# A fused two-block transformer on one core: TensorE's order at the stage ends, and the start addresses of its operands

## The chip, the cores and the metric

The kernel runs on one core of one Trainium2 chip. The metric is the device time of one launch in microseconds (us). A core has five engines that work beside each other and meet at semaphores: TensorE (in the rows PE, its weight loads PEld), VectorE (DVE), ScalarE (ACT), GpSimd (POOL) and SyncE (SP), which here issues the DMAs. A matmul holds one operand still in the array (the stationary one, at most 128x128) and streams the other one through it (the moving one, up to 512 columns); its result goes to PSUM, of which a core has eight banks of 512 float32 columns.

## The reference, cut to what matters

Two blocks of two layers each on x of 256x1024, batch 1. All matrices are float32 and are read from memory once.

```
for l in range(2):                                   # first block
    x = layer_norm(a*x + 0.5*swiglu(x, ffn1_in[l], ffn1_out[l]))          # f1
    x = layer_norm(a*x + hybrid_mixer(x, ...))                            # m1
    x = layer_norm(a*x + 0.5*swiglu(x, ffn2_in[l], ffn2_out[l]))          # f2
for l in range(2):                                   # second block
    h = rmsnorm(x); x = x + (g0*attn(h) + g1*conv(h) + g2*pool(h)) @ w_o  # m2
    h = rmsnorm(x); x = x + (silu(h@w_gate) * (h@w_up)) @ w_out           # g2

def swiglu(x, w_in, w_out):                          # d_ff = 2816
    gate, up = split(x @ w_in); return (silu(gate) * up) @ w_out
def hybrid_mixer(x, ...):                            # three attentions of 8 heads, 64 wide
    q, k, v, gates = split(x @ w_in)                 # dilated, banded, top-k
    merged = sum(sigmoid(g_i) * (o_i @ w_br_i)); return merged @ w_out
```

## The kernel before, in words

**Number format.** Every float32 operand is split in two: a high part in the matmul's own rounded format (float32r, written by ScalarE, L189) and the rest (VectorE, L190). A product is three matmuls, high by high, high by low, low by high (`mm3`, L229 to L231). In the FFN's input product (`swish_t`, L460 and L462) the activations are the moving operand, 512 columns (high and low side by side) against the weights' high part and 256 against their low part.

**Slabs.** A weight matrix is cut into slabs of 128x1024. `slab` loads one by DMA into one of 4 buffers `raw` and splits it into one of 9 slots `wh` and `wl`. A slab feeds 12 matmuls in every product. The slot comes free when the last of them has run.

**Tiles.** The activations' transpose, split, is one tile `XP` (in the rows xp): 8 blocks of 128 rows, each 256 high columns and 256 low columns. It is the stationary operand of all projections and of the output projection. The FFN's hidden tiles (ht), the attention's outputs (oh, ol) and the convolution's (cvp) are *pages*, rotating buffers of 4 KB per partition; they are the stationary operands of the FFN's output product and of the branches. VectorE, ScalarE and the DMAs are put in order by a scheduler in the build; TensorE's order is the kernel's own.

**TensorE's order.** A planner runs while the program is written. `spend` adds each matmul's expected time to a clock; `later(ns, f)` puts a piece of work (the transposes of a finished tile, an attention head's scores) into a list, due so many ns after now; when the clock passes the due time, the piece is written into TensorE's stream between two matmuls of the running product. `until` and `have` force a piece that is needed. The delays are chosen by hand: they stand for the time that the other engines need until the piece's input is there. Nothing is measured at run time: if the input is late, TensorE stands.

**Stage ends.** A stage ends with a sum over two row tiles t of 128 rows. `finish(t, O)` adds it to x, normalises (VectorE, with one power on GpSimd), and hands the transposes back to XP to `to_xt`, with a delay of 6200, 6500 or 7500 ns. In the FFN the output product of the last `TAIL` = 3 of 11 hidden units is kept for the end, as this sum: for each t, each half n of the columns, each unit u. In the mixers `branch` adds three gated products into M, and `out_project` transposes M and multiplies it by w_out.

**PSUM.** The banks are acc 3, s 2, pt 2 and tp 1. tp takes nearly all transposes and, in `attend`, also the product of weights and values.

**Addresses.** Every partition's memory is given out in the order of declaration. XP starts at byte 16,512, which is 128 past a multiple of 512. The raw, wh and wl buffers (71,456 is the first wh) and all pages (145,184 is the first) start 288 past a multiple of 512.

Of the kernel before, what the change touches and what calls it, by code (L numbers as in the profile page):

```python
# [157 lines left out]
def block_kernel(ctx: ExitStack, tc: tile.TileContext, I, out, stages=ALL):  # L158
# [79 lines left out]
        spend(360)  # L238


    XP = cpool.tile([128, 8, 2, S], F32R, name="xp")
    XH, XL = XP[:, :, 0], XP[:, :, 1]
    X = [cpool.tile([128, D], F32, name=f"x{t}") for t in range(2)]
# [10 lines left out]
    CR = cpool.tile([128, S], F32R, name="cr")  # L254
    SEL = cpool.tile([128, 8], F32R, name="sel")
    mhalf = cpool.tile([128, 8], F32, name="mhalf")
    G.memset(mhalf, -0.5)
    G.memset(CR.bitcast(F32), 0.0)

# [25 lines left out]


    def rope_tables():
        pi = cpool.tile([128, 2], I32, name="posi")
        nc.sync.dma_start(pi, I["pos"])
        pf = cpool.tile([128, 2], F32, name="posf")  # L290
        V.tensor_copy(pf, pi)
        two_pi = 2 * math.pi
        parts, rest = [], two_pi
        for _ in range(3):
            e = math.floor(math.log2(rest)) - 7
            p = math.floor(rest / 2.0 ** e) * 2.0 ** e
            parts.append(p)
            rest -= p
        parts.append(float(np.float32(rest)))
        for t in range(2):  # L300
            rt = tmp.tile([128, 4, 64], F32, tag="sm", bufs=4, name="rt")
            a, kq, b, sc = rt[:, 0, :32], rt[:, 0, 32:], rt[:, 1], rt[:, 2]
            ki = rt[:, 3, :32].bitcast(I32)
            V.tensor_scalar(a, K[:, C_INV:C_INV + 32], pf[:, t:t + 1], None, op0=OP.mult)
            V.tensor_scalar(kq, a, 1.0 / two_pi, None, op0=OP.mult)
            V.tensor_copy(ki, kq)
            V.tensor_copy(kq, ki)
            for p in parts:
                V.scalar_tensor_tensor(a, kq, -p, a, op0=OP.mult, op1=OP.add)
            V.tensor_scalar(b[:, 32:], a, math.pi, -math.pi, op0=OP.min, op1=OP.max)  # L310
            V.tensor_scalar(a, b[:, 32:], -1.0, None, op0=OP.mult)
            V.tensor_tensor(a, a, b[:, 32:], op=OP.max)
            V.tensor_scalar(b[:, :32], a, -1.0, math.pi / 2, op0=OP.mult, op1=OP.add)
            A.activation(sc, b, AF.Sin)
            for v, f in ((0, 1.0), (1, -0.125)):
                V.tensor_scalar(RT[:, v, t, 0, :32], sc[:, :32], f, None, op0=OP.mult)
                V.tensor_scalar(RT[:, v, t, 0, 32:], sc[:, :32], f, None, op0=OP.mult)
                V.tensor_scalar(RT[:, v, t, 1, :32], sc[:, 32:], -f, None, op0=OP.mult)
                V.tensor_scalar(RT[:, v, t, 1, 32:], sc[:, 32:], f, None, op0=OP.mult)
# [113 lines left out]

    def ffn(w_in, w_out, finish, prepare, started=None):
        O, H = {}, {}
        TAIL = 3

        def swish():
            h = tmp.tile([128, 2, 256], F32, tag="ropb", bufs=2, name="h")
# [68 lines left out]
            H[u] = page("op", [128, 2, 2, S], F32R, name="ht")  # L508
            split(H[u][:, 0], H[u][:, 1], p.rearrange("p b t n -> p b (t n)"))

        later(1000, lambda: h_transposes(0))
        later(5000, lambda: h_transposes(1))
        for u in range(2, NU):
            if u == 6:
                if started is not None:
# [11 lines left out]
                            out_mm(v, t, w, n)  # L527
        W = {u: out_slabs(u) for u in range(NU - TAIL, NU)}
        for t in range(2):
            for n in range(2):  # L530
                for u in range(NU - TAIL, NU):
                    out_mm(u, t, W[u], n)
            finish(t, [O[t, 0], O[t, 1]])

# [4 lines left out]
    def attend(heads, vt, vi, pen, period, sinks=None, finished=None):  # L539

        parts = [page("op", [128, 4, S], F32R, name=n) for n in ("oh", "ol")]

        def scores(pr):
            if pr < 3:
                later(period, lambda: scores(pr + 1))
            s, sm = [], []
            for hb in range(2):
                s.append(bank("s"))
                sm.append(tmp.tile([128, 386], F32, tag="sm", bufs=4, name="smx"))
            for t in range(2):  # L550
                for hb in range(2):
                    heads(2 * pr + hb, t, s[hb][:, cols(t)])
            spend(700)
            mn, den = small(4, name="mn"), small(4, name="den")
            for hb in range(2):
                h = 2 * pr + hb
                if sinks is not None:
                    V.tensor_copy(sm[hb][:, 128:386:257], sinks[:, h:h + 1].to_broadcast([128, 2]))
                for t in range(2):
                    i, c = 2 * hb + t, 129 * t  # L560
                    n = 128 * (t + 1)
                    V.tensor_tensor_reduce(
                        out=sm[hb][:, c:c + n], in0=s[hb][:, cols(t)], in1=pen(t), scale=1.0,
                        scalar=3e38 if sinks is None else sinks[:, h:h + 1],
                        op0=OP.add, op1=OP.min, accum_out=mn[:, i:i + 1])
                    if sinks is not None:
                        n += 1
                    A.activation(sm[hb][:, c:c + n], sm[hb][:, c:c + n], AF.Exp,  # L568
                                 bias=mn[:, i:i + 1], scale=-1.0, accum_out=den[:, i:i + 1])
            r = small(4, name="den")  # L570
            V.reciprocal(r, den)
            for hb in range(2):
                for t in range(2):
                    i, c = 2 * hb + t, slice(129 * t, 129 * t + 128 * (t + 1))
                    A.activation(sm[hb][:, c], sm[hb][:, c], AF.Copy, scale=r[:, i:i + 1])
            later(7500, lambda: weights(pr, sm))

        def weights(pr, sm):
            ps = []
            for hb in range(2):  # L580
                p = bank("pt")
                for b, c in enumerate((0, 129, 257)):
                    T.transpose(p[:, b * 128:b * 128 + 128], sm[hb][:, c:c + 128], ident)
                    spend(109)
                pts = tmp.tile([128, 384], F32, tag="pt", bufs=2, name="pts")
                A.activation(pts, p[:, :384], AF.Copy)
                ps.append(pts)
            later(2000, lambda: values(pr, ps))

        def values(pr, ps):  # L590
            p = bank("tp")
            for b in range(2):
                for hb in range(2):
                    v = vt[:, b, vi(2 * pr + hb), :]
                    rows = slice(hb * 64, hb * 64 + 64)
                    if b == 0:
                        T.matmul(p[rows, 0:256], v, ps[hb][:, 0:256], start=True, stop=False,
                                 skip_group_check=True)
                    else:
                        T.matmul(p[rows, 128:256], v, ps[hb][:, 256:384], start=False, stop=True,  # L600
                                 skip_group_check=True)
            spend(700)
            split(parts[0][:, pr], parts[1][:, pr], p[:, :256])
            if pr == 3:
                finished()

        scores(0)
        return parts
# [39 lines left out]
            V.scalar_tensor_tensor(y, g, 1.0, p, op0=OP.add, op1=OP.mult)  # L648
            V.tensor_tensor(m, m, y, op=OP.add)

    def branch(g, slabs, parts, M):

        w = [[slab(slabs[n, s]) for s in range(slabs.shape[1])] for n in range(2)]
        last = 2 * len(w[0]) - 1
        for t in range(2):
            ts = slice(t * 128, t * 128 + 128)
            for n in range(2):
                p = bank("acc")
                for k in range(last + 1):
                    c = slice((k % 2) * 512, (k % 2) * 512 + 512)  # L660
                    mm3(p, (parts[0][:, k, ts], parts[1][:, k, ts]),
                        (w[n][k // 2][0][:, c], w[n][k // 2][1][:, c]), k == 0, k == last)
                merge(g[n][:, t], p, None if M is None else M[n][:, t])

    def out_project(src, M, finish):

        for t in range(2):
            to_xt(t, lambda k, t=t: M[k // 4][:, t, (k % 4) * 128:(k % 4) * 128 + 128], 2500 * t)
        w = [slab(src[s]) for s in range(8)]
        for t in range(2):  # L670
            have(t)
# [7 lines left out]
    def mixer1(l, finish, prepare):  # L679
# [140 lines left out]
        branch(gb, br[1], P["b"], ga)  # L820
        prepare()
        need("c")
        branch(gc, br[2], P["c"], ga)
        out_project(I[f"w_out_{l}"], ga, finish)


    def mixer2(l, finish, prepare):
        w = I[f"w2_in_{l}"]

        def qk(src, which, name):  # L830
            tr = page("qk", [128, 4, S], name=name)

            def evac(t, p):
# [6 lines left out]
                V.tensor_scalar(ss, ss, 1.0 / HD, None, op0=OP.mult)  # L840
                r = rsqrt(ss, 8, 1e-6)
                V.tensor_tensor(qs, qs, r[:, :, None].to_broadcast([128, 8, 64]), op=OP.mult)
                later(5000, lambda: head_transposes(
                    tr, t, qs, scale=qkg[:, 2 * l + which:2 * l + which + 1]))

            return tr, (src, evac, 512)
# [143 lines left out]
        gv = [gates(w[5 + n], "o") for n in range(2)]  # L990
        prepare()
        until(lambda: "o" in ready)
        branch(gv, I[f"w2_attn_{l}"], P["o"], gt)
        out_project(I[f"w2_o_{l}"], gt, finish)


    def rms_row(kind, l):
# [19 lines left out]
    for i, (kind, l) in enumerate(stages):  # L1017
# [14 lines left out]
        def finish(t, O):  # L1032
# [14 lines left out]
                for hs in HALVES:  # L1047
                    nc.sync.dma_start(out[t, :, hs], X[t][:, hs])
            elif row is not None:
                to_xt(t, blocks(rms_norm(t, mv, rows[-1])), 7500 if first else 6500)  # L1050
            else:
                to_xt(t, blocks(X[t]), 6200)

        if kind in ("f1", "f2"):
            ffn(I[f"ffn{kind[1]}_in_{l}"], I[f"ffn{kind[1]}_out_{l}"], finish, prepare,
# [25 lines left out]
```

## Time and profile before

| | |
|---|---|
| median of 3 runs | 2052.9 us (2050.36 to 2054.67) |
| the profiled execution's own time | 2050.83 us |
| its span, first to last instruction | 2049.0 us |
| mean granted clock of TensorE | 0.998 |
| PE busy | 1998.9 us, 98% of the span |
| DVE busy | 1367.4 us, 67% |
| ACT busy | 1072.2 us, 52% |
| DMA queues' packets, share of 16 engines | 53.7% |

A matmul's recorded time (about 0.39 us for 512 columns) is from its issue to its modelled end, and the next one is issued before that. What a matmul costs in a full stream is the step from its start to the start of the next, and that is read from the timeline. A stop shows as idle time in brackets behind the instruction that waited, with the one that ended the wait.

### The profile page before, as it was taken

Reading aid. Unit: us, or ns where it says so; the run is one execution under the profiler, and the core shown is the slowest. Engines: PE = TensorE matmul, PEld = TensorE weight load, DVE = VectorE, ACT = ScalarE, POOL = GpSimd, SP = SyncE. Lnnn points to the kernel's source line nnn. Section 1 sums busy time; section 2 is a strip of 40 time slices with the busy share of each in tenths; the row PEclk is TensorE's granted clock in tenths of the full one; section 3 lists DMA queues with packets and bytes.
Section 4 is the critical chain, followed back from the end, with each engine's and each line's share of the span. In section 5 each row is a group of like instructions: output and inputs, shape, how many; then the busy total and the mean of one; then the engine's idle time right before and its main releaser. Section 6 shows DMA issues by size and latency. Waiting matters only on the chain.

```text
span 2049.0 us, 27340 instructions
## 1 busy us (share of the span) xinstructions
PE 1998.9 (98%) x10216; PEld 1636.2 (80%) x10216; DVE 1367.4 (67%) x2264; ACT 1072.2 (52%) x1767; POOL 33.8 (2%) x34
## 2 busy tenths in 40 slices
PE   8999999999999999999999999899999999999999
PEld 7888867778887888777778887778788878777887
DVE  7767775576667666885567668565666675567664
ACT  6554567635554554457735554574355545534553
POOL 0000000000000000000000000100000010000000
PEclk9999999999999999999999999999999999999999
DMA  8665544456555655543446554445465644555662
GB/s 303 222 186 169 166 134 141 137 176 225 189 191 181 199 189 167 184 139 129 145 155 236 196 185 137 161 154 196 144 206 185 195 147 141 165 175 185 186 192 85
DMA packets 99973, 358.55 MB, mean 175 GB/s; under 512 B 11904, under 2 KB 11904, under 8 KB 99840
## 3 DMA queue, kind: packets, MB, share of 16 engines
q1 hardware_dynamic: 99840, 356.81, 53.7%
q8 instruction: 80, 1.31, 0.3%
q14 instruction: 53, 0.43, 0.1%
HBM read 355.72 MB, written 1.05 MB: 174 GB/s over the span
## 4 chain that ended last, share of the span: by engine, by line
PE 83%; DVE 9%; ACT 4%; issue 2%; DMA 2%; POOL 1%; POOLq 0%; SPq 0%; DVEq 0%; ACTq 0%
PE acc L460 19%; PE acc L229 10%; PE acc L462 10%; PE acc L230 9%; PE acc L231 9%; DVE wl L190 4%; PE s L231 4%; PE s L229 3%; PE s L230 3%; PE pt L231 3%; PE pt L230 3%; PE pt L229 3%; ACT wh L189 2%; PE s L716 1%; ACT smx L568 1%
## 5 line engine op out<-in xcount | busy, mean ns | idle before, releaser
L190 DVE TENSOR_TENSOR wl<-raw,wh 128x1024 fp32r<-128x1024 f32 (+1 forms) x656 | 794.0, 1221 | 408.2 <-ACT wh L189 406.5
L189 ACT ACTIVATE wh<-raw 128x1024 fp32r<-128x1024 f32 (+1 forms) x656 | 683.7, 1055 | 592.2 <-PE pt L231 245.3
L460 PE MATMUL acc<-xp,wh 128*128 128x512 f32 x1728 | 608.9, 394 | 0.0
L462 PE MATMUL acc<-xp,wl 128*128 128x256 f32 x1728 | 482.9, 279 | 0.0
L460 PEld LDWEIGHTS acc<-xp,wh 128*128 128x128 f32 x1728 | 324.1, 188 | 76.6
L229 PE MATMUL acc<-wh,xp 128*128 128x512 f32 (+1 forms) x896 | 367.5, 410 | 6.4 <-ACT wh L189 6.4
L231 PE MATMUL acc<-wh,xp 128*128 128x512 f32 (+1 forms) x896 | 356.6, 398 | 2.5 <-DVE xp L190 2.5
L230 PE MATMUL acc<-wl,xp 128*128 128x512 f32 (+1 forms) x896 | 356.9, 398 | 0.5 <-DVE wl L190 0.5
L462 PEld LDWEIGHTS acc<-xp,wl 128*128 128x128 f32 x1728 | 324.7, 188 | 1.9
L229 PEld LDWEIGHTS acc<-wh,xp 128*128 128x128 f32 x896 | 170.5, 190 | 53.5 <-issue 11.7
L231 PEld LDWEIGHTS acc<-wh,xp 128*128 128x128 f32 x896 | 170.3, 190 | 44.5 <-DVE xp L190 4.7
L230 PEld LDWEIGHTS acc<-wl,xp 128*128 128x128 f32 x896 | 170.6, 190 | 35.9 <-DVE wl L190 1.0
L469 ACT ACTIVATE th<-gu 128x256 f32<-128x256 f32 x108 | 45.1, 417 | 136.5 <-DVE gu L466 136.4
L231 PE MATMUL s<-wh,ht 128*128 128x512 f32 x264 | 103.4, 392 | 0.7
L230 PE MATMUL s<-wl,ht 128*128 128x512 f32 x264 | 103.8, 393 | 0.0
L229 PE MATMUL s<-wh,ht 128*128 128x512 f32 x264 | 103.8, 393 | 0.0
L229 PE MATMUL pt<-wh,ht 128*128 128x512 f32 x264 | 103.2, 391 | 0.0
L231 PE MATMUL pt<-wh,ht 128*128 128x512 f32 x264 | 102.9, 390 | 0.0
L230 PE MATMUL pt<-wl,ht 128*128 128x512 f32 x264 | 102.9, 390 | 0.0
L466 DVE TENSOR_TENSOR gu<-acc,gu 128x256 f32<-128x256 f32 x216 | 90.1, 417 | 3.8 <-ACT gu L465 3.8
L465 ACT ACTIVATE gu<-acc 128x256 f32<-128x256 f32 x216 | 79.2, 367 | 5.4 <-PE acc L462 5.4
L470 DVE SCALAR_TENSOR_TENSOR h<-th,gu 128x256 f32<-128x256 f32 x108 | 45.9, 425 | 48.5 <-ACT th L469 48.5
(243 smaller groups left out, 2171.7 us busy)
## 6 DMA issues: line engine op xcount, KB each, us to landing
raw<-in_w_in_dram SPq DMA_DIRECT2D x184, 512.0 KB, 3.6
raw<-in_ffn_in_dram SPq DMA_DIRECT2D x176, 512.0 KB, 4.2
raw<-in_ffn_out_dram SPq DMA_DIRECT2D x88, 512.0 KB, 3.7
raw<-in_w_ffn_in_dram SPq DMA_DIRECT2D x88, 512.0 KB, 4.3
raw<-in_w_ffn_out_dram SPq DMA_DIRECT2D x44, 512.0 KB, 3.7
raw<-in_w_br_dram SPq DMA_DIRECT2D x24, 512.0 KB, 4.0
raw<-in_w_out_dram SPq DMA_DIRECT2D x16, 512.0 KB, 4.2
raw<-in_w_o_dram SPq DMA_DIRECT2D x16, 512.0 KB, 4.2
```

The source lines that it names most:

```text
L189: A.activation(dst_h, src, AF.Copy)
L190: V.tensor_sub(dst_l, src, dst_h.bitcast(F32))
L229: T.matmul(p, x[0], w[0], start=start, stop=False)
L230: T.matmul(p, x[0], w[1], start=False, stop=False)
L231: T.matmul(p, x[1], w[0], start=False, stop=stop)
L460: T.matmul(p, w[0][:, c], XP[:, k].rearrange("p a n -> p (a n)"), start=k == 0, stop=False, skip_group_check=True)
L462: T.matmul(p[:, 256:], w[1][:, c], XH[:, k], start=False, stop=k == 7, skip_group_check=True)
L465: A.activation(gu[:, i], p[:, 256:], AF.Copy)
L466: V.tensor_tensor(gu[:, i], p[:, :256], gu[:, i], op=OP.add)
L469: A.activation(th, gu[:, 0], AF.Tanh, scale=0.5)
L470: V.scalar_tensor_tensor(h[:, j], th, 1.0, gu[:, 0], op0=OP.add, op1=OP.mult)
L568: A.activation(sm[hb][:, c:c + n], sm[hb][:, c:c + n], AF.Exp, bias=mn[:, i:i + 1], scale=-1.0, accum_out=den[:, i:i + 1])
```

## The change

Seven edits, of which six move work in TensorE's stream and one moves tiles in memory.

- Addresses: two tiles without use (384 and 352 bytes per partition) and two small tiles declared earlier. XP then starts at byte 16,896, the slabs' first wh at 72,192 and the pages at 145,920, all multiples of 512, and so do all raw, wh, wl and page buffers.
- The FFN's kept sum: TAIL is 4, so that 8 slabs stand in the 9 slots for it, and for each t the units run outside and the halves inside.
- The weights-by-values product goes to a pt bank and is due 1000 ns later.
- `branch` itself hands out M's transposes for t when it has finished t (due 3000 ns later); `out_project` no longer does.
- The transposes of q and k in the second block's mixer are due after 9000 ns and not 5000.
- The FFN's first hidden transposes are due 1500 and 2000 ns later.
- After an FFN or a first mixer the transposes to XP are due after 7000 and not 6200 ns (no norm to come), or 10000 and not 7500 (the last FFN of the first block).

```diff
+    cpool.tile([128, 96], F32, name="pad")
     XP = cpool.tile([128, 8, 2, S], F32R, name="xp")
...
+    pi = cpool.tile([128, 2], I32, name="posi")
+    pf = cpool.tile([128, 2], F32, name="posf")
+    cpool.tile([128, 88], F32, name="pad2")
...
-        TAIL = 3
+        TAIL = 4
...
-        later(1000, lambda: h_transposes(0))
-        later(5000, lambda: h_transposes(1))
+        later(2500, lambda: h_transposes(0))
+        later(7000, lambda: h_transposes(1))
...
         for t in range(2):
-            for n in range(2):
-                for u in range(NU - TAIL, NU):
+            for u in range(NU - TAIL, NU):
+                for n in range(2):
                     out_mm(u, t, W[u], n)
...
-            later(2000, lambda: values(pr, ps))
+            later(3000, lambda: values(pr, ps))
         def values(pr, ps):
-            p = bank("tp")
+            p = bank("pt")
...
+            if last:
+                to_xt(t, lambda k, t=t: M[k // 4][:, t, (k % 4) * 128:(k % 4) * 128 + 128], 3000)
-        for t in range(2):
-            to_xt(t, lambda k, t=t: M[k // 4][:, t, (k % 4) * 128:(k % 4) * 128 + 128], 2500 * t)
...
-                later(5000, lambda: head_transposes(
+                later(9000, lambda: head_transposes(
...
-                to_xt(t, blocks(rms_norm(t, mv, rows[-1])), 7500 if first else 6500)
+                to_xt(t, blocks(rms_norm(t, mv, rows[-1])), 10000 if first else 6500)
-                to_xt(t, blocks(X[t]), 6200)
+                to_xt(t, blocks(X[t]), 7000)
```

Three places in TensorE's stream. First, the first layer's dilated attention, behind the first pair of heads (tp and pt are PSUM banks, pts the transposed weights, vx the values, ropa a rotated query that is being transposed, acc a gate's product). Before:

```order
L614 MATMUL tp_2584<-k_75,ropa_2494 128x128 x4
L229 MATMUL acc_2526<-wh_2502,xp_72 128x512
L230 MATMUL acc_2526<-wl_2503,xp_72 128x512
L231 MATMUL acc_2526<-wh_2502,xp_72 128x512
L597 MATMUL tp_2593<-pts_2549,vx_82 64x256
L597 MATMUL tp_2593<-pts_2555,vx_82 64x256
L600 MATMUL tp_2593<-pts_2549,vx_82 64x128
```

And in the changed program:

```order
L616 MATMUL tp_2586<-k_76,ropa_2496 128x128 x4
L229 MATMUL acc_2528<-wh_2504,xp_73 128x512
L230 MATMUL acc_2528<-wl_2505,xp_73 128x512
L231 MATMUL acc_2528<-wh_2504,xp_73 128x512
L229 MATMUL acc_2527<-wh_2516,xp_73 128x512
L230 MATMUL acc_2527<-wl_2517,xp_73 128x512
L231 MATMUL acc_2527<-wh_2516,xp_73 128x512
L599 MATMUL pt_2598<-pts_2551,vx_83 64x256
L599 MATMUL pt_2598<-pts_2557,vx_83 64x256
L602 MATMUL pt_2598<-pts_2551,vx_83 64x128
```

The values stand three matmuls later, and no longer in the bank that the rotated query's transposes have just filled.

Second, the end of the last branch and the start of the output projection in the first mixer (gate is M, s_3938 and s_3940 the output's sum for t = 0). Before:

```order
L231 MATMUL acc_3860<-wh_3808,ol_3313 128x512
L376 MATMUL tp_3924<-k_75,gate_2524 128x128 x4
L376 MATMUL s_3931<-k_75,gate_2859 128x128 x4
L229 MATMUL s_3938<-wh_3878,xp_72 128x512
L230 MATMUL s_3938<-wl_3879,xp_72 128x512
```

And in the changed program:

```order
L378 MATMUL tp_3866<-k_76,gate_2526 128x128 x4
L378 MATMUL s_3873<-k_76,gate_2861 128x128 x4
L229 MATMUL acc_3862<-wh_3804,oh_3314 128x512
L230 MATMUL acc_3862<-wl_3805,oh_3314 128x512
L231 MATMUL acc_3862<-wh_3804,ol_3315 128x512
L229 MATMUL acc_3862<-wh_3810,oh_3314 128x512
L230 MATMUL acc_3862<-wl_3811,oh_3314 128x512
L231 MATMUL acc_3862<-wh_3810,ol_3315 128x512
L229 MATMUL acc_3862<-wh_3810,oh_3314 128x512
L230 MATMUL acc_3862<-wl_3811,oh_3314 128x512
L231 MATMUL acc_3862<-wh_3810,ol_3315 128x512
L229 MATMUL s_3940<-wh_3894,xp_73 128x512
```

Between the transposes and the first matmul that reads their result there were none, and now there are nine.

Third, the kept sum at the end of the first FFN (s_414 and s_418 are the left half of the sum for t = 0, s_425 the right half; ht is a hidden tile). Before, the left half goes through all six slabs first:

```order
L229 MATMUL s_414<-wh_1673,ht_1404 128x512
L230 MATMUL s_414<-wl_1674,ht_1404 128x512
L231 MATMUL s_414<-wh_1673,ht_1404 128x512
L229 MATMUL s_414<-wh_1679,ht_1404 128x512
L230 MATMUL s_414<-wl_1680,ht_1404 128x512
L231 MATMUL s_414<-wh_1679,ht_1404 128x512
L229 MATMUL s_414<-wh_1685,ht_1554 128x512
```

And in the changed program:

```order
L229 MATMUL s_418<-wh_1639,ht_1256 128x512
L230 MATMUL s_418<-wl_1640,ht_1256 128x512
L231 MATMUL s_418<-wh_1639,ht_1256 128x512
L229 MATMUL s_418<-wh_1645,ht_1256 128x512
L230 MATMUL s_418<-wl_1646,ht_1256 128x512
L231 MATMUL s_418<-wh_1645,ht_1256 128x512
L229 MATMUL s_425<-wh_1639,ht_1256 128x512
L230 MATMUL s_425<-wl_1640,ht_1256 128x512
```

A unit's two slabs now serve both halves before the next unit begins, and both halves end within six matmuls of each other. For one t the kept sum has 48 matmuls, where it had 36.

## Rows read from the trace of the kernel before

**Rows 1.** The page's part 1: busy us, share of the span, instructions.

```profile
PE 1998.9 (98%) x10216; PEld 1636.2 (80%) x10216; DVE 1367.4 (67%) x2264; ACT 1072.2 (52%) x1767; POOL 33.8 (2%) x34
```

**Rows 2.** Waits of PE: line, releaser: us in total, times, longest us.

```profile
PE tp L376 <- DVE h L365: 8.0, 5, 3.0
...
PE s L231 <- DVE xp L190: 4.9, 4, 1.2
PE tp L614 <- DVE qs L842: 4.7, 4, 2.0
PE tp L597 <- ACT qb L617: 4.2, 2, 2.1
PE s L229 <- ACT xp L189: 3.0, 4, 0.8
PE tp L614 <- DVE ol L190: 2.7, 2, 1.3
PE acc L231 <- DVE xp L190: 2.5, 5, 0.9
PE tp L597 <- ACT pts L586: 1.9, 4, 0.8
PE tp L597 <- ACT qc L617: 1.7, 2, 0.9
```

**Rows 3.** Timeline of PE, kept sum, first FFN: start, us, instruction.

```profile
187.42 0.39 PE L231 MATMUL pt<-wh,ht 128*128 128x512 f32 x1
...
192.87 0.39 PE L231 MATMUL pt<-wh,ht 128*128 128x512 f32 x1
```

**Rows 4.** Timeline of PE in a branch of the first mixer.

```profile
405.70 0.39 PE L230 MATMUL acc<-wl,oh 128*128 128x512 f32 x1
...
412.50 0.39 PE L230 MATMUL acc<-wl,oh 128*128 128x512 f32 x1
```

**Rows 5.** Timeline of PE in a gate's projection.

```profile
327.99 0.40 PE L230 MATMUL acc<-wl,xp 128*128 128x512 f32 x1
...
333.85 0.40 PE L231 MATMUL acc<-wh,xp 128*128 128x512 f32 x1
```

**Rows 6.** Timeline of PE in an FFN's input product.

```profile
111.82 0.40 PE L460 MATMUL acc<-xp,wh 128*128 128x512 f32 x1
...
116.37 0.40 PE L229 MATMUL s<-wh,ht 128*128 128x512 f32 x1
```

**Rows 7.** Groups of PE by form: count | busy, mean ns | idle before.

```profile
L460 PE MATMUL acc<-xp,wh 128*128 128x512 f32 x1728 | 608.9, 394 | 0.0
...
L229 PE MATMUL acc<-wh,xp 128*128 128x512 f32 x864 | 355.2, 411 | 6.4 <-ACT wh L189 6.4
...
L229 PE MATMUL s<-wh,ht 128*128 128x512 f32 x264 | 103.8, 393 | 0.0
...
L229 PE MATMUL s<-wh,xp 128*128 128x512 f32 x64 | 26.1, 409 | 3.0 <-ACT xp L189 3.0
```

**Rows 8.** Timeline of ACT behind the first pair of heads.

```profile
276.06 0.87 ACT L586 ACTIVATE pts<-pt 128x384 f32<-128x384 f32 x2
...
280.64 0.57 ACT L617 ACTIVATE qb<-tp 128x512 f32<-128x512 f32 x1
```

**Rows 9.** Stretches: PE, PEld, DVE, ACT, POOL busy, PEclk, DMA share, GB/s.

```profile
282.00:286.00 4.00, 4.00 (x14) 3.16 (x11) 3.75 (x12) 1.81 (x6) 0.00 (x0) 0.57 0.70 213
...
1264.00:1284.00 20.00, 14.34 (x65) 10.46 (x63) 19.43 (x34) 8.23 (x10) 2.87 (x3) 1.00 0.40 137
```

**Rows 10.** Timeline of PE, start of the output projection.

```profile
424.61 0.40 PE L230 MATMUL s<-wl,xp 128*128 128x512 f32 x1
426.23 0.50 PE L231 MATMUL s<-wh,xp 128*128 128x512 f32 x1 [1.23 <-DVE xp L190]
```

**Rows 11.** Timeline of PE, first block's last FFN into the second block.

```profile
1269.18 0.66 PE L376 MATMUL tp<-k,h 128*128 128x128 f32 x4 [1.69 <-DVE h L365]
...
1283.42 0.63 PE L376 MATMUL tp<-k,h 128*128 128x128 f32 x4 [3.02 <-DVE h L365]
```

More of the change, by code (lines that the diff above doesn't have):

```diff
@@ L287, in rope_tables @@
     def rope_tables():
-        pi = cpool.tile([128, 2], I32, name="posi")
         nc.sync.dma_start(pi, I["pos"])
-        pf = cpool.tile([128, 2], F32, name="posf")
         V.tensor_copy(pf, pi)
@@ L649, in merge, with branch @@
             V.tensor_tensor(m, m, y, op=OP.add)
-    def branch(g, slabs, parts, M):
+    def branch(g, slabs, parts, M, last=False):
         w = [[slab(slabs[n, s]) for s in range(slabs.shape[1])] for n in range(2)]
-        last = 2 * len(w[0]) - 1
+        end = 2 * len(w[0]) - 1
         for t in range(2):
@@ L658, in branch, with out_project @@
                 p = bank("acc")
-                for k in range(last + 1):
+                for k in range(end + 1):
                     c = slice((k % 2) * 512, (k % 2) * 512 + 512)
                     mm3(p, (parts[0][:, k, ts], parts[1][:, k, ts]),
-                        (w[n][k // 2][0][:, c], w[n][k // 2][1][:, c]), k == 0, k == last)
+                        (w[n][k // 2][0][:, c], w[n][k // 2][1][:, c]), k == 0, k == end)
                 merge(g[n][:, t], p, None if M is None else M[n][:, t])
-    def out_project(src, M, finish):
-        for t in range(2):
-            to_xt(t, lambda k, t=t: M[k // 4][:, t, (k % 4) * 128:(k % 4) * 128 + 128], 2500 * t)
+            if last:
+                to_xt(t, lambda k, t=t: M[k // 4][:, t, (k % 4) * 128:(k % 4) * 128 + 128], 3000)
+    def out_project(src, finish):
         w = [slab(src[s]) for s in range(8)]
@@ L822, in mixer1 @@
         need("c")
-        branch(gc, br[2], P["c"], ga)
-        out_project(I[f"w_out_{l}"], ga, finish)
+        branch(gc, br[2], P["c"], ga, True)
+        out_project(I[f"w_out_{l}"], finish)
     def mixer2(l, finish, prepare):
@@ L992, in mixer2 @@
         until(lambda: "o" in ready)
-        branch(gv, I[f"w2_attn_{l}"], P["o"], gt)
-        out_project(I[f"w2_o_{l}"], gt, finish)
+        branch(gv, I[f"w2_attn_{l}"], P["o"], gt, True)
+        out_project(I[f"w2_o_{l}"], finish)
     def rms_row(kind, l):
```

## The prediction

> **What bounds the kernel now.** I read the busy times first: PE is busy 1998.9 of 2049.0 us [rows 1], so nothing but PE's own stream can give much. Two things are left in it: the 50.1 us in which it stands, and what a matmul costs while it runs. I therefore read PE's waits, then the timeline for the step from one matmul's start to the next, then the stretches for the granted clock.
>
> The nine longest waits that the edits touch hold 33.6 us in 32 stops [rows 2]. Each costs more than its idle time. At the output projection's start 1.62 us pass between two neighbours whose step is 0.23, with 1.23 us of idle shown [rows 10]: 1.39 lost, so about 0.16 us per stop on top, since a recorded matmul ends after its successor could start.
>
> The steps hold the larger surprise. With a hidden tile as the stationary operand, 24 steps take 187.42 to 192.87, 0.2271 us each [rows 3]. With an attention output, into the acc banks, 30 steps take 6.80 us, 0.2267 each [rows 4]. With xp as the stationary operand, the same instruction form, moving slabs and acc banks, 25 steps take 5.86 us, 0.2344 each [rows 5]. In the FFN's input product xp is the moving operand, and 13 pairs of 512 and 256 columns take 4.55 us, 0.350 a pair [rows 6]. So 7.3 ns, 3%, hang on xp and not on the bank. What sets xp apart in the program is its place: 128 past a multiple of 512 bytes, where slabs and pages both stand 288 past one. The change makes all of them 0.
>
> **The change part by part.** Sums are made against the profiled execution's own 2050.8 us, which lies 2.1 under the median of the three runs and inside their range.
>
> *Values in pt, 1000 ns later.* The first values of an attention wait 2.1 us for ScalarE to copy a rotated query out of the one tp bank; their own input, pts, was ready at 276.93, long before the copy ended at 281.21 [rows 8]. In a pt bank that wait has no cause. The waits of L597 (qb 4.2, pts 1.9, qc 1.7) and of L614 for ol (2.7, the reverse case) are 10.5 us in 10 stops [rows 2], 12.1 with 0.16 each. Late next: the following pair's weights need the pt bank that ol is read from. I leave 1 us for that and take 11.
>
> *M's transposes inside the branch.* Four output projections stop twice each, 3.0 and 4.9 us [rows 2], 9.2 with the surcharge. The new order puts nine matmuls, 2.0 us, between the transposes and their reader. ScalarE and VectorE do four splits in that time, and VectorE is also busy with merges and slabs; I leave 1 us and take 8. The second tile's transposes move with the first and have the whole first half of the projection as cover.
>
> *Query and key transposes after 9000 ns.* 4.7 us in 4 stops [rows 2], 5.3 in all; the input was at most 2.0 us late and gets 4. But the last of these transposes now stands straight behind the forget gate's product, which fills the same tp bank, so PE must wait until ScalarE has read it. The trace has no such pair; bounds are 0 and the 2.1 us of the nearest bank wait (qb). I take 0.7, twice. Net 4.
>
> *The FFN's ends.* The waits of L376 for h and of the first projections for xp are 8.0 and 2.5 us in 10 stops [rows 2], 12.1 in all. With 48 matmuls for a tile the first tile's norm starts 12 x 0.227 = 2.7 us earlier against the stage's end, which covers the xp waits. It does not cover all of h. Two of the five h stops stand behind an output projection whose delay stays 6500, and remain. At the seam of the two blocks VectorE is busy 19.43 of 20 us [rows 9], the two stops there are 1.69 and 3.02 [rows 11], and 10000 ns in place of 7500 changes only where PE stands. VectorE's work there does not shrink; two slab splits even move into it, because 8 kept slabs leave 1 of 9 slots free and not 3. I take 4 of 12.1; the bounds are -3 (the longer stop at this seam doubles) and 9.
>
> *Smaller stops* of the same kinds are not itemised; the hidden transposes' new delays belong here. I count 3 us.
>
> *Clock.* After the 2.1 us stop at the first values the granted clock is 0.57 over 282 to 286 [rows 9]: the lower level, 1.2 GHz, for about 3.4 us, so 1.7 us lost. Both layers have that stop, so 3.4 us in all; without the stop I expect the clock to stay, and take 3.
>
> Order and clock together: 11 + 8 + 4 + 4 + 3 + 3 = 33 us.
>
> *Addresses.* With xp stationary there are 3 x 864 + 6 x 64 = 2976 matmuls of 512 columns (three lines into acc; three lines into each of s and pt) [rows 7]. At 7.3 ns that is 21.7 us. The input product has 1728 pairs [rows 7]. A pair at equal offsets is in no row: from above, 3.1% of the whole pair, 10.9 ns, 18.8 us; from below, nothing. I take 7.3 ns, the 512-column half alone: 12.6 us. Sum 34.3, with bounds 40.5 and below zero (next part): the trace shows equal offsets only at 288, never at 0. I take the full 34 because the fast groups are just those whose two operands start at the same offset, and because they are equally fast from pages and in every bank.
>
> Total 33 + 34 = 67: 2050.8 - 67 = 1984, and I say 1983.
>
> **The rivals.**
>
> *Offsets do nothing.* Xp also differs in being one large tile low in memory, and in holding high and low parts at a stride. If that makes the 7.3 ns, only the order is left: 2050.8 - 33 = 2018. For it: no row has the same tile at two offsets. Against it: a hidden tile too holds both parts in one page, and is fast [rows 3].
> The Trainium skill speaks for this rival: "SBUF — State Buffer", section "Who interferes with whom", says that TensorE waits for nobody at memory, and "TensorE: Matmul & The Clock Gate", section "Step-by-step: what each phase is for", that loading the next weights takes no bandwidth from the running matmul. By that rule the address edit gives 0 and the time is 2018; rows 3 to 5 show a dependence on the operand for which the rule has no place.
>
> *The stops come back.* The delays are blind, and 8 kept slabs leave one slot for the next stage. If half of the 33 us return as waits for slabs or VectorE at the ten stage ends, the time is 2050.8 - 16 - 34 = 2001. For it: VectorE's 19.43 of 20 us. Against it: in the new order slabs come free in pairs over the last 48 matmuls, not in the last 18 alone.
>
> *The wrong offset, and slower.* The rows fit another reading: an operand that starts at 288 is fast and one at a multiple of 128 is slow, each adding 7.3 ns. Then all operands are slow after the change. The kept and running output sums, 6 x 264 = 1584 matmuls, lose 14.6 ns each, 23.1 us; the 2976 lose 7.3 more, 21.7; the 1728 pairs 12.6. That is +57 - 33 = +24, 2075. It is slower from the point where the mean loss over these 6288 passes 33 / 6288 = 5.2 ns. If only the fast ones join the slow, 11.6 are lost, and it ends at 2029.
>
> **How the numbers follow.** Forecast 0.57, spread 1968 to 1997 by the unknown pair and the stage ends. Offsets do nothing 0.24 (2012 to 2024). Stops come back 0.11 (1995 to 2008). Wrong offset 0.08, half of it at 2029, half slower. Repeats differ from no change by about 0.2%, 4 us. Only the last half case is slower: 0.04; within 0.2% I give 0.02 for mixtures; faster 0.94. The range reaches from 1966 over the second rival and most of the first, to 2022.
>
> **What would show it.** Steps at xp of 0.227 and pairs of 0.343 or less confirm the addresses; 0.234 refutes them, and steps above 0.228 in the kept sum mean the wrong offset. No wait of the values (L599 in the changed kernel) for a rotated query, none of the output projection above 0.5 us, and no stretch below full clock confirm the order; h waits of 5 us at the seam or new waits for wh or wl at stage starts refute its size. The prediction is wrong if the time lies above 2022.

## The result, and the profile after

The changed kernel takes 2005.7 us (median of 4 runs, 2004.8 to 2008.4) against 2051.6 in the same session, a ratio of 0.9775 (95% interval 0.9763 to 0.9787). It is 46 us faster; 67 were forecast. The profiled execution's own time is 2005.5 us at a span of 2003.7.

Part 1 of the page, changed kernel:

```profile
PE 1976.7 (99%) x10216; PEld 1634.0 (82%) x10216; DVE 1364.1 (68%) x2264; ACT 1072.3 (54%) x1767; POOL 30.2 (2%) x34
```

PE's idle time fell from 50.1 us (2049.0 - 1998.9, [rows 1]) to 2003.7 - 1976.7 = 27.0. Its waits in the changed kernel (us in total, times, longest):

```profile
PE tp L378 <- DVE h L367: 9.1, 5, 2.9
PE acc L229 <- ACT wh L189: 6.1, 1, 6.1
PE tp L616 <- DVE qs L845: 3.8, 1, 3.8
PE tp L616 <- ACT ft L879: 1.1, 2, 0.6
PE pt L599 <- ACT pts L588: 1.0, 2, 0.5
PE tp L378 <- DVE x L354: 0.6, 1, 0.6
PE tp L378 <- issue: 0.6, 1, 0.6
PE acc L230 <- DVE wl L190: 0.5, 1, 0.5
```

Beside [rows 2]: the waits for a rotated query (qb, qc) and for ol are gone, and so are all those of the output projection (s L229, s L231) and of the first projections (acc L231). The h waits have grown from 8.0 to 9.1 us. The four stops for qs, 2.0 us at most, have become one of 3.8. The 1.1 us for ft is the new wait behind the forget gate's product, 0.55 each where 0.7 was forecast. The 6.1 us for the first slab is the launch and was there before [rows 7].

The timeline of PE for the steps, changed kernel (start, us from issue to modelled end, instruction), an FFN input product and then a gate's projection:

```profile
104.41 0.39 PE L462 MATMUL acc<-xp,wh 128*128 128x512 f32 x1
...
115.34 0.40 PE L462 MATMUL acc<-xp,wh 128*128 128x512 f32 x1
...
437.70 0.39 PE L229 MATMUL acc<-wh,xp 128*128 128x512 f32 x1
...
444.96 0.40 PE L231 MATMUL acc<-wh,xp 128*128 128x512 f32 x1
```

With xp stationary, 32 steps take 7.26 us, 0.2269 each, where 0.2344 stood [rows 5]: xp is now as fast as a page. But 31 pairs of the input product take 10.93 us, 0.3526 a pair, and the pair was 0.350 [rows 6]. It did not fall; it rose.

The stretches behind the first values and behind the new stop for qs (busy us of PE, PEld, DVE, ACT and POOL; PEclk, the granted clock as a share of full speed; DMA share, GB/s):

```profile
280.00:286.00 6.00, 6.00 (x35) 4.64 (x33) 5.84 (x14) 5.76 (x13) 0.00 (x0) 1.00 0.61 188
...
1652.00:1658.00 6.00, 6.00 (x25) 4.70 (x26) 2.54 (x5) 1.69 (x3) 1.64 (x1) 0.72 0.58 216
```

Full clock where 0.57 was granted [rows 9], but 6 x (1 - 0.72) = 1.7 us lost behind the stop for qs.

### The profile page after: what moved, and what is told of

It reads as the page before. It is cut to its first block, busy times and chain, and to the rows that moved or that the text cites. A ratio compares the mean times of both kernels' runs of the same rounds, so it can differ in the third digit from the quotient of the medians.

```text
span 2003.7 us, 27312 instructions
## 1 busy us (share of the span) xinstructions
PE 1976.7 (99%) x10216; PEld 1634.0 (82%) x10216; DVE 1364.1 (68%) x2264; ACT 1072.3 (54%) x1767; POOL 30.2 (2%) x34
## 4 chain that ended last, share of the span: by engine, by line
PE 92%; DVE 4%; ACT 1%; issue 1%; DMA 1%; POOL 0%; POOLq 0%; SPq 0%; ACTq 0%; DVEq 0%
PE acc L462 20%; PE acc L229 11%; PE acc L231 11%; PE acc L230 11%; PE acc L464 10%; PE s L231 4%; PE s L229 4%; PE s L230 4%; PE pt L231 3%; PE pt L229 3%; PE pt L230 3%; DVE wl L190 1%; PE s L719 1%; PE pt L585 1%; PE pt L599 1%
## 5 line engine op out<-in xcount | busy, mean ns | idle before, releaser
L229 PE MATMUL acc<-wh,xp 128*128 128x512 f32 (+1 forms) x896 | 362.2, 404 | 6.1 <-ACT wh L189 6.1
L231 PE MATMUL acc<-wh,xp 128*128 128x512 f32 (+1 forms) x896 | 350.9, 392 | 0.0
L230 PE MATMUL acc<-wl,xp 128*128 128x512 f32 (+1 forms) x896 | 350.0, 391 | 0.5 <-DVE wl L190 0.5
L229 PEld LDWEIGHTS acc<-wh,xp 128*128 128x128 f32 x896 | 169.2, 189 | 49.5 <-issue 12.1
L231 PEld LDWEIGHTS acc<-wh,xp 128*128 128x128 f32 x896 | 169.1, 189 | 36.2
L229 PE MATMUL s<-wh,ht 128*128 128x512 f32 x264 | 103.8, 393 | 0.0
L231 PE MATMUL s<-wh,ht 128*128 128x512 f32 x264 | 103.2, 391 | 0.0
L229 PE MATMUL pt<-wh,ht 128*128 128x512 f32 x264 | 103.2, 391 | 0.0
L231 PE MATMUL pt<-wh,ht 128*128 128x512 f32 x264 | 102.7, 389 | 0.0
```

What stands on the lines that cost most here:

```text
L229: T.matmul(p, x[0], w[0], start=start, stop=False)
L230: T.matmul(p, x[0], w[1], start=False, stop=False)
L231: T.matmul(p, x[1], w[0], start=False, stop=stop)
```

## The experiments

In the runs on addresses and on the alternation, the theories are told apart by the same reading: the xp-stationary step and the pair, the one over 28 to 32 steps of the timeline, the other over 31 pairs. The runs on stops are read by PE's waits. Edits are shown in part, with the cuts marked by dots, against the changed kernel.

**The order alone.** The two idle tiles leave and the two small ones go back; XP stands at 128, slabs and pages at 288 again.

```
-    cpool.tile([128, 96], F32, name="pad")
...
-    cpool.tile([128, 88], F32, name="pad2")
...
```

> The changed kernel without the address edit: xp at 128, slabs and pages at 288 past a multiple of 512. Theory A (the address edit gives the 2976 matmuls with xp stationary 7.2 ns each, 21 us, and costs the input product's 1728 pairs about 2.5 ns each, 4 us): 2005.7 + 17 = 2023 us, steps at stationary xp 0.234 us, pairs 0.3505. Rival O (the order alone made the gain): 2006 us, steps 0.227.

Measured: 2015.8 us (2015.0 to 2016.5), 0.9817 (0.9801 to 0.9832), 37 us less than the 2053.0 of before. PE's busy time, its stop for qs, and its timeline:

```profile
PE 1988.2 (99%) x10216; PEld 1633.8 (81%) x10216; DVE 1364.9 (68%) x2264; ACT 1073.5 (53%) x1767; POOL 30.2 (2%) x34
...
PE tp L614 <- ACT sq L838: 2.5, 1, 2.5
...
104.19 0.40 PE L460 MATMUL acc<-xp,wh 128*128 128x512 f32 x1
...
115.05 0.39 PE L460 MATMUL acc<-xp,wh 128*128 128x512 f32 x1
...
250.44 0.40 PE L230 MATMUL acc<-wl,xp 128*128 128x512 f32 x1
...
257.00 0.39 PE L231 MATMUL acc<-wh,xp 128*128 128x512 f32 x1
```

0.3503 a pair and 0.2343 a step, both as before, as theory A says of the steps. So the order gives the 33 us and a little more, and the addresses only 10 on top of it (9 by the two ratios), where theory A had 17 and rival O nothing. The late stop for qs is already there with the order alone.

**The addresses alone.** All of the order is as before (delays, banks, loops); the pads and the two moved declarations stay.

```
-        TAIL = 4
+        TAIL = 3
...
-                later(9000, lambda: head_transposes(
+                later(5000, lambda: head_transposes(
...
```

> The kernel before with the address edit alone. Theory A: 2051.6 - 17 = 2035 us, steps at stationary xp 0.227, pairs 0.353, waits of PE as before (33.6 us in the nine rows). Rival O: 2052 us.

Measured: 2049.8 us (2044.0 to 2052.8), 0.9979 (0.9967 to 0.9990): almost nothing where theory A had 2035, though its steps are as A says: 28 xp-stationary steps from 251.35 to 257.73 take 0.2279 each. The second stop at the start of the output projection, and two of its stretches:

```profile
423.58 0.59 PE L231 MATMUL s<-wh,xp 128*128 128x512 f32 x1 [1.23 <-DVE xp L190]
...
422.00:430.00 8.00, 6.77 (x27) 5.25 (x26) 4.54 (x7) 1.14 (x3) 0.00 (x0) 0.79 0.58 190
...
1264.00:1276.00 12.00, 9.96 (x32) 7.29 (x33) 11.87 (x20) 3.52 (x5) 1.47 (x2) 0.72 0.41 132
```

and one of the kernel before, the same output projection:

```profile
423.00:431.00 8.00, 6.01 (x32) 4.57 (x31) 6.20 (x9) 2.79 (x5) 0.00 (x0) 1.00 0.79 235
```

Behind the output projection's stop, 1.23 us in both [rows 10], the clock now falls to its lower level and did not before. Five more such stretches of 8 us at 0.79 lie at 279, 910, 1473, 1828 and 1862 us. Together they lose 6 x 8 x 0.21 + 12 x 0.28 = 13.4 us, and the kernel before lost 3.4 in its two (0.57 over 282 to 286 [rows 9], 0.79 over 909 to 917). PE's idle time grew too, from 50.1 to 2048.0 - 1994.5 = 53.5 us. The ten runs agree with this: the three whose mean granted clock was 0.996 or 0.997 took 2044.0 to 2046.0 us, 7 to 9 under the kernel before, and the seven at 0.992 to 0.995 took 2049.4 to 2052.8. The steps' gain was there and was given back behind the old order's stops, mostly as clock; why the same stop is now followed by a lower clock stays open.

**Where XP starts.** Four kernels move XP against the slabs, and one puts everything at another start.

```
-    cpool.tile([128, 96], F32, name="pad")
+    cpool.tile([128, 112], F32, name="pad")
...
-    cpool.tile([128, 88], F32, name="pad2")
+    cpool.tile([128, 72], F32, name="pad2")
```

This moves XP, and with it the small tiles declared between the two pads, by 64 bytes and leaves slabs and pages where they are; 104 and 80 move it by 32, 128 and 56 by 128, 160 and 24 by 256. The fifth kernel has pad at 40 and pad2 at 88, so that XP, slabs and pages all start at 288.

> The changed kernel with xp (and the constants) 64 bytes past a multiple of 512, slabs and pages at 0 as in the change. Theory E (the step depends on the two operands starting at the same place modulo 512): steps at stationary xp back to 0.234, 2027 us if the pairs stay at 0.353. Rival R (it is enough that every operand starts at a multiple of 64): 0.227, 2006 us.

> The changed kernel with xp, slabs and pages all 288 past a multiple of 512, equal but at no multiple of 64. Theory E (equality counts): steps at stationary xp 0.227, time near 2006 us. Rival R (the multiple of 64 or 512 counts): 0.234 or more at stationary xp, 2027 us or more.

> The changed kernel with XP 256 bytes off the slabs' starts modulo 512 (all else as after the change). Known so far: at 0 an XP-stationary 512 takes 0.2270 us and a pair of the FFN input product 0.3528; at 64, 0.2334 and 0.3492; at 160 (the kernel before), 0.2342 and 0.3503. Theory E (only an equal start modulo 512 is fast for stationary XP, any other costs the same): 0.234 and 0.349 to 0.351, so 2012 us. Rival H (a start half a line away is as good as an equal one): 0.227 and 0.353, 2006 us.

> The changed kernel with XP 32 bytes off the slabs' starts modulo 512. Theory E (only an equal start is fast for stationary XP): 0.234 us, with the pair at 0.349 to 0.351 as at 64 and 160, 2012 us. Rival G (the price grows with the distance): 0.230 for stationary XP and a pair between 0.349 and 0.353, 2007 us.

> The changed kernel with XP 128 bytes off the slabs' starts modulo 512. At 0 and at 256 stationary XP took 0.2270 us (median) and a pair 0.353; at 32, 64 and 160 it took 0.232 to 0.234, a pair 0.347 to 0.350. Theory 256 (the distance counts modulo 256): 128 is as far as it can be, 0.233 to 0.234, 2010 us. Rival 128 (it counts modulo 128): 0.2270 and 0.353, 2006 us.

The times below the first row are medians of two runs each, which lie at most 2.5 us apart; that of the order alone is of four.

| XP's start less the slabs' | xp stationary, us a step | input product, us a pair | time, us |
|---|---|---|---|
| 0 (the changed kernel) | 0.2269 | 0.3526 | 2005.7 |
| 0, all at 288 | 0.2269 | 0.3529 | 2006.8 |
| 32 | 0.2332 | 0.3474 | 2007.9 |
| 64 | 0.2332 | 0.3490 | 2011.8 |
| 128 | 0.2332 | 0.3506 | 2012.0 |
| 256 | 0.2266 | 0.3529 | 2006.4 |
| 352, that is 96 modulo 256 (order alone) | 0.2343 | 0.3503 | 2015.8 |

The steps at 0 and 256 are read over 32 unbroken steps, at 437 us in the changed kernel, the others over 28 steps behind four transposes, at 250 us. At the latter place the 28 steps take 0.2275 each in the changed kernel and 0.2279 at 256, so the gap is smaller there but stays. Over the whole traces, all steps under 0.3 us between two xp-stationary matmuls (2686 to 2704 in each) have means of 0.2280 at 0 and at 256, 0.2332 at 32, 0.2334 at 64, 0.2327 at 128 and 0.2342 in the order alone.

The rows at 256:

```profile
103.95 0.39 PE L462 MATMUL acc<-xp,wh 128*128 128x512 f32 x1
...
114.89 0.40 PE L462 MATMUL acc<-xp,wh 128*128 128x512 f32 x1
...
437.65 0.39 PE L229 MATMUL acc<-wh,xp 128*128 128x512 f32 x1
...
444.90 0.40 PE L231 MATMUL acc<-wh,xp 128*128 128x512 f32 x1
```

and at 32:

```profile
104.74 0.40 PE L462 MATMUL acc<-xp,wh 128*128 128x512 f32 x1
...
115.51 0.39 PE L462 MATMUL acc<-xp,wh 128*128 128x512 f32 x1
...
250.44 0.39 PE L230 MATMUL acc<-wl,xp 128*128 128x512 f32 x1
...
256.97 0.40 PE L231 MATMUL acc<-wh,xp 128*128 128x512 f32 x1
```

What counts is the distance between the two operands' starts, not a round address (288 is as good as 0). It counts modulo 256: my theory of 512 fell with the run at 256, and the run at 128 shows that the period is no shorter. That the price grows with the distance (rival G) is refuted too: 32 bytes already cost the whole step. And the pair goes the other way: distance 0 is its slowest, and 32, under every forecast for it, its fastest of those tried. So E's 2027 at 64 was 15 us too high, and the time at 32 came out where G had it. Some expectations write 160 for the place of the kernel before; that is the same distance with the other sign.

**The alternation.** The same multiplications, another order inside a tile.

```
                     for k in range(8):
                         T.matmul(p, w[0][:, c], XP[:, k].rearrange("p a n -> p (a n)"),
                                  start=k == 0, stop=False, skip_group_check=True)
+                        spend(236)
+                    for k in range(8):
+                        c = slice(k * 128, k * 128 + 128)
                         T.matmul(p[:, 256:], w[1][:, c], XH[:, k], start=False, stop=k == 7,
                                  skip_group_check=True)
-                        spend(353)
+                        spend(117)
```

> The changed kernel, with one thing moved: in the FFN input product the eight 512-column multiplications of a tile run first, then its eight 256-column ones, where they alternated. After the change a pair takes 0.3528 us (0.2360 + 0.1168), 1728 pairs. Theory L (the price lies in the alternation: the weight load for the long one, 188 ns in the trace, does not fit beside a 256-column stream of 113 ns, and the long one pays): the 512s among themselves go at the 0.227 of every other 512, the 256s at the 0.118 to 0.120 that they take back to back in the projections with slab weights; 0.346 a pair, 12 us less: 1994 us. Rival M (the price belongs to XP as the moving operand at the same start as the weights, whoever stands next): the 512s stay at 0.236, the sum at 0.353, 2005 us; if the 256s now wait for loads of 188 ns each, 0.42 a pair and 2120 us.

Measured: 1998.3 us (1997.0 to 2001.7), 0.9723 (0.9709 to 0.9738). Its timeline of PE, eight to a row:

```profile
502.16 2.00 PE L462 MATMUL acc<-xp,wh 128*128 128x512 f32 x8
504.00 1.12 PE L467 MATMUL acc<-xp,wl 128*128 128x256 f32 x8
504.96 2.00 PE L462 MATMUL acc<-xp,wh 128*128 128x512 f32 x8
```

Here eight 512s take 1.84 us, 0.230 each, eight 256s 0.96, 0.120 each: 0.350 a pair. Over the 204 unbroken groups of the trace the mean is 0.3486 a pair, 4.2 ns under the 0.3528 of the expectation, and 1728 x 0.0042 = 7.3 us is what the run gained. Theory L had 0.346. XP as the moving operand is thus not slow by itself, which refutes theory M; but the 512s don't reach 0.227 on average. In these groups the steps behind the first five 512s have means of 0.228 to 0.234, and only those behind the last three 0.2267. The changed kernel shows the same with xp stationary, where projections go on behind four transposes:

```profile
250.27 0.39 PE L230 MATMUL acc<-wl,xp 128*128 128x512 f32 x1
...
251.66 0.39 PE L230 MATMUL acc<-wl,xp 128*128 128x512 f32 x1
...
256.64 0.39 PE L231 MATMUL acc<-wh,xp 128*128 128x512 f32 x1
```

The first 6 steps take 1.39 us, 0.2317 each; the next 22 take 4.98, 0.2264 each. With unequal starts the steps never settle: 0.2343 over the whole of this place in the order alone. So the fast step comes only after some unbroken 512-column steps with operands at distance 0. The input product, broken by a 256 at every second instruction, never gets there, so it has nothing to gain from distance 0. Why it even loses there against 32 or 96 is not shown.

**Grouped, with XP at 32.** Pads of 104 and 80 in the kernel above.

> The grouped order (eight 512s, then eight 256s of a tile) with XP 32 bytes off the slabs' starts modulo 512. Measured so far: grouped at 0, 512s 0.2295 us (median 0.228), 256s 0.120; alternating at 32, 0.2288 and 0.1183, XP-stationary 512s 0.2332, 256s back to back in the projections with slab weights 0.117 (median). Theory R (what counts is how far the running address of the stream is from that of the load beside it, modulo 256, whichever of the two is XP, so that every 512 behind a 512 wants 0): the grouped 512s go up to 0.232 or more, the 256s down to 0.117, a pair 0.349 to 0.350, XP-stationary 0.233: 2012 us. Rival S (a moving XP wants 32 and a stationary XP 0): the grouped 512s stay at 0.228, 256s 0.117, a pair 0.345: 2005 us.

Measured: 2017.3 us (two runs, 2017.3 and 2017.4). Its timeline:

```profile
660.49 2.03 PE L462 MATMUL acc<-xp,wh 128*128 128x512 f32 x8
662.35 1.09 PE L467 MATMUL acc<-xp,wl 128*128 128x256 f32 x8
```

1.86 us for eight 512s, 0.2325 each: without distance 0 the grouped ones do not settle either, whichever operand XP is. Over 204 groups the 512s have a mean of 0.2335, the 256s 0.1174, a pair 0.3509. So R's steps hold, its pair nearly, and S falls; the time is 5 us above R's figure, and the running address by which R explains them was not tested.

**The stops that were left.** Where does the new 3.8 us come from? DVE in the changed kernel around it, with rows left out:

```profile
1636.25 0.17 DVE L327 TENSOR_SCALAR rsy<-ss 128x8 f32<-128x8 f32 x1
1638.24 0.69 DVE L845 TENSOR_TENSOR qs<-qs,rsr 128x512 f32<-128x512 f32 x1 [1.82 <-POOL rsr L329]
1638.86 4.62 DVE L190 TENSOR_TENSOR wl<-raw,wh 128x1024 fp32r<-128x1024 f32 x4
1643.39 0.68 DVE L842 TENSOR_REDUCE ss<-sq 128x8 f32<-128x512 f32 x1
1645.49 1.23 DVE L190 TENSOR_TENSOR wl<-raw,wh 128x1024 fp32r<-128x1024 f32 x1 [1.41 <-ACT wh L189]
...
1651.08 0.69 DVE L845 TENSOR_TENSOR qs<-qs,rsr 128x512 f32<-128x512 f32 x1 [0.38 <-POOL rsr L329]
```

and SP's queue:

```profile
1626.20 1.12 SPq L860 DMA_DIRECT2D pws<-in_pool_s_dram  x2
1640.10 20.17 SPq L194 DMA_DIRECT2D raw<-in_w_in_dram  x9
```

DVE waits 1.82 us for POOL's power; four low parts of slabs queue behind the product and free the raw buffers late; SP issues nothing until 1640.1; and the next low part, for which DVE then stands, is ahead of the third qs. This experiment takes the product from DVE and lets h fall due later:

```
-                V.tensor_tensor(qs, qs, r[:, :, None].to_broadcast([128, 8, 64]), op=OP.mult)
+                G.tensor_tensor(qs, qs, r[:, :, None].to_broadcast([128, 8, 64]), op=OP.mult)
...
-                to_xt(t, blocks(rms_norm(t, mv, rows[-1])), 10000 if first else 6500)
+                to_xt(t, blocks(rms_norm(t, mv, rows[-1])), 13000 if first else 8500)
```

> The changed kernel with two orders changed: the product of qs with its norm goes from DVE to POOL, and the transposes of h fall due 8500 ns (13000 behind the last FFN) after the sum instead of 6500 (10000). Theory B (DVE stands still while it waits for POOL's power, the slabs' low parts queue behind that, SP cannot refill, and the third qs comes 3.8 us late at 1647 us): the stop there goes, with the half clock behind it (1.7 us), and the h stops of 3.1, 1.9, 1.3 and 1.9 us fall to 0.5 or less: about 12 us less, 1994 us. Rival D (the slabs are late there by the transfers themselves, and the h stops move to the next boundary): the qs stop stays at 3 us or more, the h stops come back before the second token tile, 2002 to 2006 us; POOL's product may also be so much slower than DVE's 0.69 us that the q and k transposes stop, 2010 us.

Measured: 2004.2 us (2004.1 to 2006.5), 0.9753 (0.9737 to 0.9769), no change from the changed kernel and in rival D's range. PE's waits:

```profile
PE acc L231 <- DVE xp L190: 9.0, 1, 9.0
...
PE tp L616 <- POOL qs L845: 1.3, 1, 1.3
...
PE tp L378 <- DVE h L367: 0.9, 1, 0.9
```

The qs stop falls from 3.8 to 1.3 us and the h stops from 9.1 to 0.9, as B says. But at the seam of the blocks a stop of 9.0 us is new, with the granted clock at 0.57 over the 12 us from 1246. There the 13000 put the first tile's transposes behind the second tile's last product; DVE did most of the second tile's norm first and split the first tile's xp after it. So B holds for its stops, and D in that a stop moved on.

**Both, without the 13000.** The grouped order, qs on POOL, 8500; 10000 at the seam as in the changed kernel.

> The grouped order, with the product of qs on POOL, and h due 8500 ns after the sum behind the output projections (10000 behind the last FFN, as after the change). If the terms add: 1998.3 (grouped) less the h stops of 2.1, 2.0 and 1.9 us, less 2.5 of the qs stop and 1.7 to 3.4 of half clock behind it: 1989 us (1986 to 1993). If the stops only move on, as the 13000 did in the run before: 1996 to 1998.

Measured: 1990.2 us (1989.1 to 1993.9), 0.9698 (0.9673 to 0.9723) of before, the fastest here and 15 us under the changed kernel. PE's waits:

```profile
PE tp L378 <- DVE h L367: 4.5, 2, 2.9
PE tp L619 <- POOL qs L848: 1.9, 2, 1.7
```

The terms add; the two h stops left are those of the seam, and with 10000 there the 9.0 us stop is gone. The grouped kernel with the product on DVE still has the qs stop at 3.6 us, here its longest is 1.7: this pair of runs bears out the cause without the 9.0 us stop in between.

**Four delays more.** As the last, with 10500 for q and k, 8500 for x, 3000 for the forget gate, 3800 for the values.

> As the run before, with four more delays longer: q and k transposes 10500 ns (9000), x behind the first FFNs and the mixers 8500 (7000), the forget gate's transposes 3000 (2000), the values 3800 (3000). They aim at stops of 1.3 (qs), 0.7 and 0.7 (x), 0.8 and 0.8 (forget), 0.65 and 0.65 (values). If each gets its wait covered: 4 to 5 us less than the run before, 1985. Rival: the later transposes make their readers late (the x of the second token tile, the probabilities' product), and it is the same or up to 5 us longer.

Measured: 1991.9 us (1989.2 to 1994.3), 0.9700 (0.9679 to 0.9721): no difference. The rival held. The x stops went, and the next transposes now wait 2.8 us for xp; the values' went, and the next weights wait 1.0 us for smx; and with 10500 in place of 9000 the one qs stop left is 2.7 us, where the longest was 1.7.

## Why the prediction was right, and where it was not

The range, wide enough for the rivals, holds the time; the forecast's own spread, 1968 to 1997, does not. The time is nearest to the rival "the stops come back" (2001), but that is not what happened: the order gave its 33 us and more, and the addresses gave 10 of 34. That the time lies in a rival's spread is luck.

- *Values.* 10.5 us in 10 stops became 1.0 in 2, which is 10.8 with the surcharge of 0.16 a stop; 11 were forecast.
- *M's transposes.* All 7.9 us are gone, 9.2 with the surcharge; 8 were forecast.
- *Queries and keys.* Forecast 4, measured 0. 4.7 us in 4 stops became 3.8 in one and 1.1 in two at the forget bank. That price was right. What failed is "the input was at most 2.0 us late and gets 4": the lateness of an input is not fixed. In the new order the second layer's third qs came behind slabs that DVE and SP had in their queues. The product on POOL took it to 1.3 (in the grouped kernels from 3.6 to 1.7), so its place in DVE's queue is shown as the larger part of it; the rest is not split further.
- *FFN ends.* The xp waits went (2.5 us) as said; the h waits rose by 1.1. With the surcharge 2.2 us, where 4 were taken within -3 to 9. The seam stayed nearly as it was, as said: 1.58 and 2.90 us, after 1.69 and 3.02 [rows 11]. PE at the seam, changed kernel:

```profile
1239.80 0.66 PE L378 MATMUL tp<-k,h 128*128 128x128 f32 x4 [1.58 <-DVE h L367]
...
1255.26 0.63 PE L378 MATMUL tp<-k,h 128*128 128x128 f32 x4 [2.90 <-DVE h L367]
```

- *Clock.* 3 were taken; two half-clock stretches went (3.4 us) and one came behind qs (1.7), so 1.7 were gained. The forecast's sign "no stretch below full clock" was not met.
- *The order's sum.* 37 us by its own run against 33. The four terms and the clock above hold 24. Of the smaller stops, 3 in the forecast, 3.8 us in 7 went, 4.9 with the surcharge. The other 8 are not split: with the order alone PE's idle time fell by 25.2 us, to 2013.1 - 1988.2 = 24.9, and its busy time by 10.7, more in both than these terms hold. So it is in part luck that the sum came out near.
- *Xp stationary.* 21.7 us were forecast at 7.3 ns. Rows of long runs show 7.4 (0.2343 to 0.2269), so the size per step was right where a run is long. Steps behind a break gain less: at the place above, 28 steps gain 6.56 - 6.37 = 0.19 us, 6.8 ns each, and over the whole traces the mean falls from 0.2342 to 0.2280, 6.2 ns, which is 18.5 us for the 2976. My sum took every step as settled, 3 us too many.
- *The input product: the step that failed.* It stood at 7.3 ns a pair, 12.6 us, "the 512-column half alone". Measured, it is +2.3 to +2.6 ns, so 1728 x 0.0025 = 4 us lost: 17 of the 24 us by which the addresses fell short. Of the other 7, 3 are the steps that had not settled, and 2 stand as idle time of PE, 27.0 us where the order alone has 24.9; the rest is not split. I took "equal is fast" from rows of unbroken 512-column runs and carried it to a stream broken by a 256 each time. The pair's bound from below, "nothing", was wrong too: no row excluded a loss there.

The rival "offsets do nothing" is refuted by the sweep, the same tile at several places. With only XP and its neighbours moved, 28 steps at the same place take 0.2332 us each at 128 bytes and 0.2279 at 256. By "SBUF — State Buffer" of the Trainium skill, section "Who interferes with whom", TensorE waits for nobody at memory, and the two would be equal; the traces do not agree, and the measurement decides, though no run shows that it is at memory that the time is lost. "The wrong offset" is refuted by the changed kernel itself, whose operands all start at 0 and whose steps are 0.2269, and by the run with all at 288, which is no faster. What in the chip makes the distance count was not measured and stays open.

## What to carry to other kernels

Read the step from start to start, by what is stationary and what moves, and try a shift of a few hundred bytes: it costs nothing but padding. Judge it by the steps and the granted clock as well as by the time: here it gave 10 us with the new order and almost nothing in the median without it. A figure from one pattern of instructions holds for that pattern; where a stream is broken by shorter matmuls, measure it. Before a delay is made longer, ask what stands in the queue of the engine that produces the input: of the delays tried, those that moved a wait to the next reader gave nothing.

## What the runs showed of the hardware

- In this kernel a 512-column float32r matmul steps at 0.2266 to 0.2269 us when both operands start at the same place modulo 256 bytes, and at 0.233 to 0.234 on average at the unequal distances tried (32, 64, 96, 128). At equal starts it takes some steps after each break to get there (0.2317 over six).
- 256-column ones, back to back at distance 0, step at 0.120, more than half of the 512's; an alternating pair costs 0.3474 to 0.3529 by the distance.
- The same stop of 1.23 us was followed by full clock in one kernel and by a mean of 0.79 over 8 us in another, whose steps were faster.
